# Decoder block on one core: the two attention masks loaded apart, the modulation's later pieces given to DVE or POOL in mixer B's units, staging places for x of their own

## The chip, the cores and the metric

The kernel runs on one core of a Trainium2 chip. Its time is device microseconds of one execution; the median of three runs of the kernel before is 1162.92 us (1161.84 to 1165.6). A core has TensorE (PE, with its weight loads as PEld), VectorE (DVE), ScalarE (ACT), GpSimd (POOL) and SyncE (SP), which issues the DMAs here. Each engine works through its own list of instructions in order and waits at an instruction until the semaphores that it names are reached.

## The reference

One layer of a transformer block, batch 1, 1024 tokens, width 1024, all in float32:

```python
mod = cond @ w_ada + b_ada                     # six vectors: shift, scale, gate, twice
h = rms_norm(x, g_attn_pre) * (1 + sc_a) + sh_a
proj = h @ w_in                                # q, k, v of mixer A and of mixer B
oa = banded_attention(qa, ka, va, 127, sink)   # 8 query heads, 2 key heads, window 128
ob = dilated_mixture_attention(qb, kb, vb)     # 8 heads, windows 128/1, 512/4, 2048/16
mixed = concatenate([rms_norm(oa, g_mix_a), rms_norm(ob, g_mix_b)])
x = x + gt_a * rms_norm(mixed @ w_out, g_attn_post)
h = rms_norm(x, g_mlp_pre) * (1 + sc_m) + sh_m
x = x + gt_m * rms_norm(square(relu(h @ w_up)) @ w_down, g_mlp_post)
```

`cond` is silu of the conditioning vector; q and k are partly rotated by position (rope) before the attention.

## The kernel before

Each float32 product is made of three passes on PE, with operands split into a high and a low part (`hi` by ACT, `lo` by DVE or POOL): in the projection these are L859, L860 and L862. The program is written by a planner in Python (`Sched`): steps are put in with their engine (or a choice of two), a planned duration, what they depend on, which places they take and give, and a priority. The planner keeps a clock for every engine and every DMA and writes out one fixed order for each engine. So a changed duration, priority or number of places moves instructions on all engines.

The stages, with the times of the profiled execution:

- *Prologue*, to about 60 us: norm of x, the first two of the six modulation vectors, the modulated input `hw`.
- *Input projection with attention*, to about 415 us. Six units u: 0 and 1 make the heads of mixer A, 2 to 5 those of mixer B. A unit has two halves x of 512 tokens and three chunks c (`proj_tile`: eight steps of three matmuls into `pj`). `evac` carries a chunk off: chunk 0 is rotated (DVE L755 to L758, with tables `tab` that ACT fills from `ptab`), the others are split by ACT (`hl`, L772) and DVE (L775) into a staging tile `hl`; SP scatters its rows to `kt` and `qt` (L801), some twelve DMAs a half. Values go over `vt` (ACT L823) and PE's transposes `pv` (L829). The attention runs between the matmuls of later chunks: scores `s_ps` (L1175 for A, L1120 for B), mask and maximum on DVE (L1190, L1139), exp on ACT, the scaling of the probabilities on POOL (L1207, L1151), transposes `pt_ps`, their split `ph` (ACT L1239, DVE L1243), `o_ps` (L1255, L1267) and `ot`, which SP stores to `o_dram`.
- *The rest of the modulation.* `feed_ada` puts in 24 pieces (`ada_piece`), four for each of six halves of vectors. A piece loads 512 KB of `w_ada` (`wa_st`, L992) into a staging tile and adds its two rows, times `cond`, to `ada_acc`. On POOL that takes two instructions for a row (L1007, L1008; L1003 begins a sum); a form for DVE with one instruction (L1005) exists and is used for eight more pieces in the MLP.
- *Output projection*, to about 550 us: eight blocks of 128 tokens (`out_block`): `y_ps` (L1471 to L1473), norm, times the gate (L1514), plus x (L1517, x loaded at L1420), norm, `xn` (ACT L1525), transposes `px` (L1534). `load_wo` loads `w_out` before it.
- *MLP*, to the end: seven products of half-size blocks in place of eight, eight parts; PE is filled here.

What orders the work around the change: the staging tiles of 4 KB per partition (`stage`, resource `r_stg`, five places while the projection runs) are shared by `hl`, `wa_st`, the rope rows and others. The masks of both mixers lie side by side in `masks` (1024 columns for B, 256 for A) and are loaded by one DMA (L969) when `open_attention` runs. In the output projection the staging places were tiles of the ring `ring_r`, opened by `open_h2` after the last attention step.

## Time and profile before

| | us |
|---|---|
| median of three runs | 1162.92 |
| the profiled execution | 1165.66 |
| its span, first to last instruction | 1163.9 |
| PE busy | 1116.5 |
| DVE busy | 818.9 |
| ACT busy | 639.2 |
| POOL busy | 260.9 |

The mean granted clock of PE is 0.986. The page gives an engine's busy time and its share of the span; a row of waits gives the engine and line that waited, what came last, the total, the times and the longest; a timeline row gives start, length, engine, line, instruction and, in brackets, the idle time before it. Since PE is busy for nearly all of the span, the reading goes by the few places where it is not, and by the clock that it is granted there.

### The profile page before, as it was taken

The page shows a single profiled execution, that of the slowest core. Times are in us where ns is not written, and L with a number is a line of the kernel's source. Part 1 is how long each engine was busy: PE and PEld are TensorE (multiplying, and loading weights), DVE is VectorE, ACT ScalarE, POOL GpSimd, SP SyncE. Part 2 cuts the span into 40 slices and gives each one's busy share as a digit, 9 for nine tenths or more (in the row PEclk, how much of TensorE's full clock was granted, in tenths as well). Part 3 has the DMA queues.
Part 4 walks back from the last instruction along what each step waited for, and adds up shares of the span by engine and source line. Part 5 has one row for each costly group of instructions (what it writes and reads, how often), then busy time and mean ns, then how long its engine had stood idle before and what let it go on. Part 6 is the DMA issues. An engine that isn't in the chain of part 4 may idle for free.

```text
span 1163.9 us, 15646 instructions
## 1 busy us (share of the span) xinstructions
PE 1116.5 (96%) x5416; PEld 925.9 (80%) x5416; DVE 818.9 (70%) x1380; ACT 639.2 (55%) x1105; POOL 260.9 (22%) x344
## 2 busy tenths in 40 slices
PE   9979989899999999998999999999999999999996
PEld 7768767788888777887788888888888888888885
DVE  7848667666666775668969665499653796647998
ACT  7939676445456674667666524563234732246542
POOL 2337766656562441112000000000000000000002
PEclk9989989999999989999999999999999999999998
DMA  9577847565555523564683157912369312584103
GB/s 335 175 161 168 168 108 186 114 150 114 137 117 136 137 66 131 175 205 181 228 321 123 34 188 267 331 55 91 111 216 329 113 55 73 181 302 186 37 19 145
DMA packets 90944, 185.31 MB, mean 159 GB/s; under 512 B 8432, under 2 KB 31088, under 8 KB 90864
## 3 DMA queue, kind: packets, MB, share of 16 engines
q1 hardware_dynamic: 90864, 184.30, 51.8%
q8 instruction: 43, 0.70, 0.3%
q14 instruction: 37, 0.30, 0.1%
HBM read 137.08 MB, written 28.31 MB: 142 GB/s over the span
## 4 chain that ended last, share of the span: by engine, by line
PE 69%; DVE 10%; DMA 6%; issue 5%; ACT 4%; POOL 4%; SPq 1%; DVEq 0%; POOLq 0%; ACTq 0%
PE mlp_ps L1896 16%; PE mlp_ps L1897 16%; PE mlp_ps L1895 16%; PE pj L859 3%; PE pj L862 3%; PE pj L860 3%; PE s_ps L1120 2%; DMA qt<-hl 2%; PE o_ps L1255 1%; PE pt_ps L1225 1%; PE pt_ps L1228 1%; DMA w_st<-in_w_in 1%; DMA x_sb<-in_x 1%; DVE hw L1666 1%; PE y_ps L1471 1%
## 5 line engine op out<-in xcount | busy, mean ns | idle before, releaser
L1895 PE MATMUL mlp_ps<-hw 128*128 128x512 f32 x896 | 349.7, 390 | 1.2 <-ACT hw L1657 1.2
L1896 PE MATMUL mlp_ps<-hw 128*128 128x512 f32 x896 | 348.7, 389 | 1.1 <-DVE hw L1663 1.1
L1897 PE MATMUL mlp_ps<-hw 128*128 128x512 f32 x896 | 348.6, 389 | 0.0
L1895 PEld LDWEIGHTS mlp_ps<-hw 128*128 128x128 f32 x896 | 168.2, 188 | 36.8 <-ACT hw L1657 1.6
L1896 PEld LDWEIGHTS mlp_ps<-hw 128*128 128x128 f32 x896 | 168.2, 188 | 36.6 <-DVE hw L1663 1.4
L1897 PEld LDWEIGHTS mlp_ps<-hw 128*128 128x128 f32 x896 | 168.2, 188 | 35.0
L1666 DVE TENSOR_TENSOR hw<-w,hw 128x1024 fp32r<-128x1024 f32 x96 | 114.7, 1221 | 93.5 <-ACT hw L1659 93.3
L1659 ACT CAST hw<-w 128x1024 fp32r<-128x1024 f32 x96 | 97.4, 1047 | 129.8 <-PE mlp_ps L1897 97.5
L1995 POOL TENSOR_TENSOR st<-st,nhalf 128x1 f32<-128x1 f32 x8 | 7.8, 978 | 601.9 <-DVE st L1993 601.9
L859 PE MATMUL pj<-hw,w_hl 128*128 128x512 f32 x240 | 103.8, 433 | 0.0
L862 PE MATMUL pj<-hw,w_hl 128*128 128x512 f32 x240 | 95.2, 397 | 0.0
L860 PE MATMUL pj<-hw,w_hl 128*128 128x512 f32 x240 | 94.8, 395 | 0.0
L1243 DVE TENSOR_TENSOR ph<-pt_ps,ph 128x512 fp32r<-128x512 f32 (+1 forms) x110 | 69.8, 648 | 34.8 <-ACT ph L1239 34.3
L1659 ACT CAST hw<-u 128x1024 fp32r<-128x1024 f32 x48 | 48.7, 1052 | 64.6 <-PE mlp_ps L1897 64.6
L1239 ACT CAST ph<-pt_ps 128x512 fp32r<-128x512 f32 (+1 forms) x110 | 59.4, 555 | 31.6 <-PE pt_ps L1228 26.5
L1146 ACT ACTIVATE p_sb<-p_sb,mn 128x128 f32<-128x128 f32 (+3 forms) x64 | 49.8, 778 | 37.6 <-DVE mn L1139 36.2
L1666 DVE TENSOR_TENSOR hw<-u,hw 128x1024 fp32r<-128x1024 f32 x48 | 57.1, 1220 | 18.2 <-ACT hw L1659 18.2
L1953 DVE TENSOR_TENSOR yacc<-yacc,mlp_ps 128x512 f32<-128x512 f32 x96 | 62.2, 683 | 3.3 <-PE mlp_ps L1897 3.3
L1151 POOL TENSOR_SCALAR p_sb<-p_sb,den 128x128 f32<-128x128 f32 (+3 forms) x64 | 48.5, 767 | 49.0 <-DVE den L1149 45.7
L1008 POOL TENSOR_TENSOR ada_acc<-ada_acc,wa_st 128x512 f32<-128x512 f32 x42 | 55.0, 1310 | 3.5
L862 PEld LDWEIGHTS pj<-hw,w_hl 128*128 128x128 f32 x240 | 45.5, 189 | 10.6
L1471 PE MATMUL y_ps<-hw,oh 128*128 128x512 f32 x128 | 51.7, 404 | 0.0
(205 smaller groups left out, 2014.4 us busy)
## 6 DMA issues: line engine op xcount, KB each, us to landing
hw<-s_dram SPq DMA_DIRECT2D x84, 512.0 KB
wa_st<-in_w_ada SPq DMA_DIRECT2D x32, 512.0 KB
w<-in_w_up SPq DMA_DIRECT2D x32, 512.0 KB
w<-in_w_down SPq DMA_DIRECT2D x32, 512.0 KB
s_dram<-hw SPq DMA_DIRECT2D x28, 512.0 KB
w_st<-in_w_in SPq DMA_DIRECT2D x36, 256.0 KB
x_sb<-in_x SPq DMA_DIRECT2D x16, 512.0 KB
wa<-in_w_ada SPq DMA_DIRECT2D x32, 256.0 KB
```

Of the source, the lines that this page charges most:

```text
L859: T.matmul(ps, w[:, 0, n], h[0], start=(k == 0), stop=False)
L860: T.matmul(ps, w[:, 1, n], h[0], start=False, stop=False)
L862: T.matmul(ps, w[:, 0, n], h[1], start=False, stop=(k == KC - 1))
L1239: A.copy(b["ph"][:, 0, :w], b["pt"][:, :w])
L1243: V.tensor_tensor(b["ph"][:, 1, :w], b["pt"][:, :w], b["ph"][:, 0, :w].bitcast(F32), ALU.subtract)
L1471: T.matmul(ps[:], b["oh"][:, k], wh[:, c0:c0 + 512], start=(k == 4 * m), stop=False)
L1659: A.copy(out[j][0], flat(src[j]))
L1666: V.tensor_tensor(out[j][1], flat(src[j]), out[j][0].bitcast(F32), ALU.subtract)
L1895: T.matmul(ps[m][:], sh, mh, start=starts and k == 0, stop=False, **kw)
L1896: T.matmul(ps[m][:], sh, ml_, start=False, stop=False, **kw)
L1897: T.matmul(ps[m][:], sl, mh, start=False, stop=k == 3, **kw)
L1953: e = op("DVE", t_dv(512), lambda: V.tensor_tensor(y(), y(), ps[m][:], ALU.add), [e, ml.e_y[tb, n]], gives=gives, prio=1)
```

## The change

1. The mask of A (256 columns, 128 KB) is loaded alone when the attention opens; that of B (1024 columns, 512 KB) when chunk (1, 1, 0) of the projection is put in.
2. The planner counts 1.9 times the bytes for a scatter to `kt` and `qt`.
3. The 24 pieces are put in from 1.9 units on, over 3.3 units (before: from 1.0, over 4.1), and each may go to DVE or to POOL (before: POOL).
4. `load_wo` may begin with three chunks left instead of two.
5. The four staging places of the output projection are a pool of their own (`stg2`), opened by `open_out`, which starts the output projection; the ring on the right has 20 tiles instead of 24, and `open_h2` gives no staging places any more.

```diff
@@ -440,8 +440,6 @@
     def stage(name):
-        if st.stgp is None:
-            return ring_r(name)
         return st.stgp.tile([P, 1024], F32, name=name, tag="stg")
@@ -808,7 +806,7 @@
                             posted()
-                    by = sum(a[1] * 2048 * (4 if both else 1) for a in mine)
+                    by = 1.9 * sum(a[1] * 2048 * (4 if both else 1) for a in mine)
                     e = load(f_st, by, [eh if s_ == 0 else el] + ([] if new else [e_new[u, x]]),
@@ -941,6 +939,9 @@
                 next_unit_w(u)
+            if (u, x, c) == (1, 1, 0):
+                e_mask.append(load(lambda: nc.sync.dma_start(masks[:, :1024], consts[:, CW_MB:CW_MB + 1024]), 524288,
+                                   prio=-9))
             if (u, x, c) == (2, 0, 0):
@@ -953,7 +954,7 @@
             return False
-        nonlocal kring, qring, pprob, pth, opool, adp, mask_a, mask_b, e_mask
+        nonlocal kring, qring, pprob, pth, opool, adp, masks, mask_a, mask_b, e_mask
         right0.close()
@@ -966,14 +967,14 @@
         masks = mkp.tile([P, 1280], F32, name="masks")
-        e_mask = load(lambda: nc.sync.dma_start(masks[:], consts[:, CW_MB:CW_MB + 1280]), 655360, prio=-20)
+        e_mask = [load(lambda: nc.sync.dma_start(masks[:, 1024:], consts[:, CW_MA:CW_MA + 256]), 131072, prio=-20)]
         mask_b = masks[:, 0:1024]
...
 
-    kring = qring = pprob = pth = opool = adp = mask_a = mask_b = e_mask = None
+    kring = qring = pprob = pth = opool = adp = masks = mask_a = mask_b = e_mask = None
     sc.launch += [feed_proj, open_attention]
@@ -993,7 +994,7 @@
 
-        def f_acc():
+        def f_acc(eng):
             wa = ada.raw.pop(i)[:].rearrange("p (j n) -> p j n", j=2)
@@ -1006,8 +1007,9 @@
                     G.tensor_tensor(ada.acc[:, :512], ada.acc[:, :512], wa[:, j], ALU.add)
-        e = op("DVE" if eng is V else "POOL", 1.2 if eng is V else 3.64, f_acc,
-               [el, ada.e], takes=[(r_acc or r_adacc, 1)] if jp == 0 else [], gives=[(r_stg, 1)], prio=9)
+        engs = (("DVE",), (1.3,), (lambda: f_acc(V),)) if eng is V else (
+            ("DVE", "POOL"), (1.3, 3.97), (lambda: f_acc(V), lambda: f_acc(G)))
+        e = op(*engs, [el, ada.e], takes=[(r_acc or r_adacc, 1)] if jp == 0 else [], gives=[(r_stg, 1)], prio=9)
         ada.e = e
@@ -1059,8 +1061,8 @@
     def feed_ada():
-        if st.d > 1.0 + ada.i * 4.1 / NADA and ada.i < NADA:
-            ada_piece(ada.i, G, lambda: adp.tile([P, 512], F32, name="ada_acc", tag="ada_acc", bufs=1), lambda: px.tile([P, 512], F32, name="ada_ps", tag="x"), r_x)
+        if st.d > 1.9 + ada.i * 3.3 / NADA and ada.i < NADA:
+            ada_piece(ada.i, None, lambda: adp.tile([P, 512], F32, name="ada_acc", tag="ada_acc", bufs=1), lambda: px.tile([P, 512], F32, name="ada_ps", tag="x"), r_x)
             ada.i += 1
@@ -1139,7 +1141,7 @@
                                            mn[:, 0:1] if m else BIG, ALU.add, ALU.min, mn[:, m:m + 1])
-                last_mn = op("DVE", t_dv(cw) + (AP_DV if m else 0), f_max, [e, e_mask] + ([last_mn] if m else []), gives=[(r_s, 1)], prio=1)
+                last_mn = op("DVE", t_dv(cw) + (AP_DV if m else 0), f_max, [e, e_mask[1]] + ([last_mn] if m else []), gives=[(r_s, 1)], prio=1)
 
@@ -1194,7 +1196,7 @@
                                  scale=-1.0, accum_out=b["den"][:, h:h + 1])
-                em = op("DVE", t_dv(256 - k0) + 0.16, f_max, [e, es, e_mask], gives=[(r_s, 1)] if hh else [], prio=1)
+                em = op("DVE", t_dv(256 - k0) + 0.16, f_max, [e, es, e_mask[0]], gives=[(r_s, 1)] if hh else [], prio=1)
                 ea.append(op("ACT", t_sb(256 - k0) + 2 * AP_COST, f_exp, [em], prio=1))
@@ -1331,7 +1333,7 @@
 
-        if len(todo_dense) > 2 or ada.i < NADA:
+        if len(todo_dense) > 3 or ada.i < NADA:
             return False
@@ -1362,13 +1364,14 @@
         ph2.left = pool("ring_l", 10)
-        st.stgp = None
         r_stg.free.clear()
...
         ph2.junk = pool("junk2", 1).tile([P, D], BF16, name="junk2")
+        st.stgp = pool("stg2", NSTG2)
+        r_stg.give(sc.clk["PE"], NSTG2)
         ph2.tb = 0
@@ -1381,8 +1384,7 @@
         rightv.close()
-        ph2.right = pool("ring_r", 24, "right")
-        r_stg.give(sc.clk["PE"], NSTG2)
+        ph2.right = pool("ring_r", 20, "right")
         r_raw.give(sc.clk["PE"], 10)
```

What this does to the order, at three places on which the prediction rests. First SP, where it has loaded the first weights and begins to scatter the keys and queries of unit 0, half 0. Before:

```order
L528 DMA w_st<-in_w_in 128x512 x6
L969 DMA masks<-in_consts 128x1280
L528 DMA w_st<-in_w_in 128x512
L992 DMA wa_st<-in_w_ada 128x2x512
L801 DMA kt<-hl 64x2x512 x2
L801 DMA qt<-hl 8x4x512 x4
```

Now:

```order
L526 DMA w_st<-in_w_in 128x512 x6
L970 DMA masks<-in_consts 128x256
L526 DMA w_st<-in_w_in 128x512
L799 DMA kt<-hl 64x2x512 x2
L799 DMA qt<-hl 8x4x512 x4
```

The load of the modulation is gone from ahead of `kt`, and the masks' load is a fifth as wide. The other 1024 columns stand now behind both halves' scatters and two loads of weights of unit 1. On PE three `pj` matmuls and the first four `pv` now stand ahead of the first scores instead of behind them.

Second SP again, at the scatter of unit 1, half 1. The number behind a name tells tiles apart: `hl_1457`, `hl_1598` and `hl_1748` are the staging tiles of chunks 0, 1 and 2 before. Before:

```order
L801 DMA qt_1520<-hl_1457 8x4x512 x4
L528 DMA w_st_1577<-in_w_in 128x512
L1312 DMA o_dram3_113<-ot_1531 64x2x128 x2
L1048 DMA gate_d0_80<-gate_st_1412 128x512
L801 DMA qt_1520<-hl_1598 24x4x512
L801 DMA qt_1520<-hl_1598 8x4x512
L992 DMA wa_st_1624<-in_w_ada 128x2x512
L801 DMA qt_1520<-hl_1598 24x4x512
L801 DMA qt_1520<-hl_1598 8x4x512
L528 DMA w_st_1665<-in_w_in 128x512
L992 DMA wa_st_1741<-in_w_ada 128x2x512
L801 DMA qt_1520<-hl_1748 16x4x512
```

Now, where `hl_1470`, `hl_1569` and `hl_1694` are those tiles:

```order
L799 DMA qt_1527<-hl_1470 8x4x512 x4
L799 DMA qt_1527<-hl_1569 24x4x512
L799 DMA qt_1527<-hl_1569 8x4x512
L526 DMA w_st_1598<-in_w_in 128x512
L1314 DMA o_dram3_113<-ot_1571 64x2x128 x2
L799 DMA qt_1527<-hl_1569 24x4x512
L799 DMA qt_1527<-hl_1569 8x4x512
L526 DMA w_st_1647<-in_w_in 128x512
L993 DMA wa_st_1656<-in_w_ada 128x2x512
L799 DMA qt_1527<-hl_1694 16x4x512
```

The first of all `wa_st` loads now stands behind the last store of chunk 1; before, two stood in this stretch, one between the stores of chunk 1.

Third the pieces of the modulation in unit 2. POOL before, where `w_hl` is the low part of a weight tile and `p_sb` are probabilities:

```order
L542 TENSOR_TENSOR w_hl<-w_st,w_hl 128x512
L1007 TENSOR_SCALAR wa_st<-wa_st,cond 128x512
L1008 TENSOR_TENSOR ada_acc<-ada_acc,wa_st 128x512
L1007 TENSOR_SCALAR wa_st<-wa_st,cond 128x512
L1008 TENSOR_TENSOR ada_acc<-ada_acc,wa_st 128x512
L1166 COPY p_sb<-nsink 128x4
L1207 TENSOR_SCALAR p_sb<-p_sb,den_1769 128x256 x4
```

DVE now, at its second piece (`mn` is the row maximum with the mask, `den` the sum):

```order
L1192 ISA p_sb,mn_1932<-s_ps,masks,nsink 128x256
L1192 ISA mn_1932 128x1
L1201 RECIPROCAL den_1933<-den_1933 128x4
L1006 SCALAR_TENSOR_TENSOR ada_acc<-wa_st,cond,ada_acc 128x512 x2
L1245 TENSOR_TENSOR ph<-pt_ps,ph 128x512
L1192 ISA p_sb,mn_2050<-s_ps,masks,nsink 128x256
L1192 ISA mn_2050 128x1
```

Four instructions on POOL have become two on DVE, between the steps of the attention. Of the 24 pieces 19 are on DVE and five on POOL.

In the output projection SP's load of x for block 0 stands right behind the load of that block's attention output (`o_sb`); before, it stood behind six more stores and a second `o_sb`. PE's order in the MLP is the same.

## The prediction

> **What bounds the kernel now.** I began with the page's busy times, then the stages (windows), then the waits of TensorE, and last the timeline at each long wait.
>
> ```profile
> PE 1116.5 (96%) x5416; PEld 925.9 (80%) x5416; DVE 818.9 (70%) x1380; ACT 639.2 (55%) x1105; POOL 260.9 (22%) x344
> ```
>
> TensorE (PE) has work for 96% of the span. So the change can win only idle time of PE and half-clock time of PE. The stages say where those are; the columns are the stretch, its length, the busy time of PE, PEld, DVE, ACT and POOL (with counts), the granted clock, the DMA share and GB/s.
>
> ```profile
> 155.00:385.00 230.00, 223.99 (x1265) 189.01 (x1264) 152.51 (x389) 130.21 (x284) 133.98 (x149) 1.00 0.57 133
> 60.00:155.00 95.00, 81.64 (x430) 67.47 (x429) 57.43 (x166) 61.50 (x169) 59.92 (x101) 0.92 0.76 161
> ```
> ```profile
> 570.00:600.00 30.00, 30.00 (x134) 24.86 (x133) 22.43 (x22) 18.34 (x26) 0.00 (x0) 1.00 0.90 337
> ```
>
> The MLP (from 570 us) leaves no gap in such a row. Units 0 and 1 (60 to 155 us) lose 95 - 81.64 = 13.4 us, and the clock of 0.92 costs about 7 more; units 2 to 5 (155 to 385 us) lose 6 us. The waits of PE name the causes (total, times, longest):
>
> ```profile
> PE s_ps L1175 <- DMA kt<-hl: 7.3, 1, 7.3
> PE px L1534 <- ACT xn L1525: 5.7, 3, 3.1
> PE pv L829 <- ACT tab L719: 5.2, 1, 5.2
> PE pv L829 <- DVE ot L1291: 3.2, 2, 2.8
> ```
>
> The change touches the first three of them: the first scores' wait for scattered keys and queries (7.3), the wait behind ACT at 146 us (5.2), and one of the three waits for `xn` in the output projection.
>
> **The masks and the first scores.** SP's timeline (start, length, instruction) shows the scatter behind a load of the modulation (the masks' load is the DMA but one before it), and PE's what waits for it; the third fence has the DMA share and rate in three stretches of 2 us, the fourth the granted clock:
>
> ```profile
> 65.03 0.44 SPq L992 DMA_DIRECT2D wa_st<-in_w_ada  x1
> 67.65 1.78 SPq L801 DMA_DIRECT2D kt<-hl  x2
> 69.49 8.23 SPq L801 DMA_DIRECT2D qt<-hl  x10
> ```
> ```profile
> 77.25 0.39 PE L862 MATMUL pj<-hw,w_hl 128*128 128x512 f32 x1
> 84.97 1.94 PE L1175 MATMUL s_ps<-kt,qt 128*128 128x128 f32 x8 [7.33 <-DMA kt<-hl]
> ...
> 88.09 0.63 PE L859 MATMUL pj<-hw,w_hl 128*128 128x512 f32 x1
> ...
> 89.51 0.69 PE L829 MATMUL pv<-head,vt 64*128 64x64 f32 x4
> 90.12 1.74 PE L1175 MATMUL s_ps<-kt,qt 128*128 128x256 f32 x8
> ```
> ```profile
> 66.00:68.00 2.00, 2.00 (x11) 1.65 (x10) 1.92 (x4) 1.74 (x4) 1.48 (x2) 1.00 1.03 380
> 72.00:74.00 2.00, 2.00 (x10) 1.65 (x9) 0.14 (x1) 0.00 (x0) 1.92 (x3) 1.00 0.58 93
> 78.00:80.00 2.00, 0.00 (x0) 0.00 (x0) 0.00 (x0) 0.44 (x1) 0.00 (x0) 1.00 0.99 153
> ```
> ```profile
> 81.08:84.49 3.41, 0.00 (x0) 0.00 (x0) 0.63 (x1) 0.00 (x0) 0.00 (x0) 0.50 0.77 124
> 84.49:87.91 3.42, 2.94 (x11) 2.78 (x12) 3.34 (x10) 1.10 (x2) 0.43 (x1) 0.50 0.66 134
> 87.91:91.32 3.41, 3.41 (x13) 2.45 (x13) 0.64 (x5) 2.52 (x11) 2.41 (x6) 0.50 0.78 136
> ```
>
> The order now puts only 128 KB of mask ahead of the scatter. Mask B (128 x 1024 x 4 bytes) and the first `wa_st` (as much) leave the queue: 1.05 MB, at the 380 GB/s of 66 to 68 us 2.8 us of transfer. That is the most the scatter can come earlier. The least is nothing: the last scatter is issued at 69.49 + 8.23 = 77.7 us whatever lies ahead, and at 72 to 74 us the DMA engines were only 0.58 busy, waiting for issue. I take 2.0, nearer to the upper end since at 78 to 80 us they were full (0.99) and still worked off the queue.
>
> Second, PE's order now has three more `pj` matmuls and the four `pv` ahead of the first scores. They stood behind them at half clock: 89.51 - 88.09 = 1.4 for the three and 90.12 - 89.51 = 0.6 for the four, so 1.9 to 2.0 us, now hidden in the wait. I count 1.9.
>
> Third, the clock. It was 0.50 from 81.08 to 91.32 us: full speed came only after a window in which PE had 3.41 of 3.41 us. If the scores start at about 83, the window 84.49 to 87.91 is full and the next is fast: 3.41/2 = 1.7 won. I take 1.1, as the wait stays over 4 us and the drop itself remains. **Sum: -2.0 - 1.9 - 1.1 = -5.0 us**, from -1.9 (transfers no earlier) to -6.4. In these rows the drop goes with a long idle stretch of PE. The Trainium skill, TensorE: Matmul & The Clock Gate, Part 1, says that the gate watches a free-running window of about 3.4 us and halves the clock after an idle one; the rows agree (steps of 3.41 us). By that rule a wait shortened below a window would keep the clock and this part would be some 2 us better still.
>
> **Mask B and the modulation's pieces out of unit 1.** ACT's waits from 120 to 156 us, SP's timeline, the chain and the clock:
>
> ```profile
> ACT hl L772 <- DMA qt<-hl: 5.1, 1, 5.1
> ```
> ```profile
> 135.49 0.44 SPq L992 DMA_DIRECT2D wa_st<-in_w_ada  x1
> ```
> ```profile
> 137.66 9.39 DMA qt<-hl
> ```
> ```profile
> 149.35:152.76 3.41, 0.93 (x5) 0.81 (x6) 2.73 (x9) 3.36 (x11) 3.24 (x5) 0.50 0.49 125
> 152.76:156.17 3.41, 3.41 (x14) 3.12 (x14) 1.50 (x6) 1.09 (x4) 3.37 (x8) 0.50 0.38 89
> ```
>
> ACT's `hl` of unit 1 needs a stage place. Five exist and the order has two `wa_st` loads among that half's stores, the first of them above, so it waits for the scatter of the chunk before (9.39 us, with 512 KB loads in the same queue). Everything behind it on ACT is late by 5.1 us, and PE with it (5.2), then PE works 0.93 + 3.41 = 4.3 us at half clock, which is 2.2 us lost. In the new order no `wa_st` is issued until the last scatter of that chunk, and the `hl` takes a place that the chunk before the last gave back. At best the whole 5.2 + 2.2 = 7.4 goes; what is late next is ACT's own queue. **I take -6.5**, range -7.4 to -3. Mask B's load (512 KB) now stands in unit 1, ahead of that unit's scatter; the scores that need it are in unit 2, tens of microseconds later, so I cost it at nothing. If it delays that scatter, the price is its transfer, 1.4 us at 380 GB/s.
>
> **The pieces on DVE.** POOL did 24 pieces of two steps each in units 1 to 5 and DVE does 19 of them now, at units 2 to 5. The rows of before, by line (min/median/max ns); the DVE row is of the pieces that it does in the MLP:
>
> ```profile
> L1007 POOL TENSOR_SCALAR wa_st<-wa_st,cond x42: 686/698/1129, 72.4 to 338.4; 128x512 f32<-128x512 f32 x42
> L1008 POOL TENSOR_TENSOR ada_acc<-ada_acc,wa_st x42: 1269/1296/1615, 73.2 to 339.2; 128x512 f32<-128x512 f32 x42
> ...
>   DMA wa_st<-in_w_ada: 34.5, 9
> ```
> ```profile
> L1005 DVE SCALAR_TENSOR_TENSOR ada_acc<-wa_st,cond,ada_acc x14: 746/752/753, 630.8 to 784.4; 128x512 f32<-128x512 f32 x14
> ```
> ```profile
> DVE ot L1291 <- DMA o_dram<-ot: 3.8, 1, 3.8
> ```
>
> 19 x 2 x 0.75 = 28.5 us at most come to DVE, and 19 x 2 x (0.70 + 1.30) = 76 us leave POOL. From 155 to 385 us DVE was busy 152.5 of 230; it will be 181, or 79%. That is cover, but DVE keeps its order: behind a piece stand, in the new order, `ot`, `ph` and the masked scores; PE waits for `ph`, ACT for the scores, and both wait out a piece (1.5 us), and its load too if that is late. POOL sat 34.5 us, in 9 waits, for these loads, at little cost to PE. How a DVE wait reaches PE one row pair shows: DVE waited 3.8 for a DMA, PE 2.8 for that `ot` (0.74 of it). Bounds: -2 (of the 6 us that PE lost there a freer POOL, which scales the probabilities for the transposes, wins back a third), +8 (11 us of DVE delays reach PE at 0.74). **I take +2**: the loads are now placed after the scatters, which get 1.9 times the planned cost, and PE lost only 6 us there in all.
>
> Now the row on which a rule bears that speaks against the move:
>
> ```profile
> L542 DVE TENSOR_TENSOR w_hl<-w_st,w_hl x14: 674/692/1247, 18.2 to 309.5; 128x512 fp32r<-128x512 f32 x14
> ```
>
> Some DVE steps with two SBUF inputs took up to 1247 ns for 692, while the median is undisturbed. The Trainium skill, SBUF — State Buffer, Who interferes with whom, says that a DVE instruction with two SBUF inputs and a GpSimd instruction that reads SBUF shut each other out for the whole instruction; the pieces are of that kind. What it would do here is the fifth rival.
>
> **Places for x.** In block 0 of the output projection the sum with x waits for x:
>
> ```profile
> 447.46 1.27 DVE L1514 SCALAR_TENSOR_TENSOR y_sb<-y_sb,st,gate_a 128x1024 f32<-128x1024 f32 x1
> ...
> 453.38 1.22 DVE L1517 TENSOR_TENSOR y_sb<-y_sb,x_sb 128x1024 f32<-128x1024 f32 x1 [1.67 <-DMA x_sb<-in_x]
> ```
> ```profile
> 458.45 1.09 PE L1534 MATMUL px<-head,xn 128*128 128x128 f32 x8 [2.17 <-ACT xn L1525]
> ```
>
> `y_sb` is ready at 448.73, x comes at 453.3, PE stands 2.17 us for what follows. With places from the start of the output projection, SP loads x right behind the block's `o_sb`, ahead of six stores that it used to follow. The 4.6 us go, and PE's 2.2 us with them; next late is ACT's `xn`, covered by the matmuls of block 1. **-2.2**, range 0 to -2.3. That `load_wo` may start one chunk earlier and that the second ring has 20 tiles I cost at nothing: PE's order in the MLP is the same, and the MLP rows have no gap.
>
> **Sum.** -5.0 - 6.5 - 2.2 + 2.0 = -11.7. The profiled execution took 1165.66 (span 1163.9 and 1.8 around it), 2.7 above the median of the three runs; its waits are all in the program's order, so I take the difference from the median: 1162.92 - 11.7 = **1151.2 us**.
>
> **The rivals.**
> 1. *Slower: DVE takes over POOL's waits for `wa_st`.* 34.5 x 19/24 = 27.3 us of DVE waits in units 2 to 5, at 0.74: 20.2 us of PE against 13.7 gained, **1169.4 us**. It decides from 13.7/0.74 = 18.5 us of DVE waits on. For it: DVE's first step of each piece waits for the load itself. Against: DMA share there is only 0.57, and the pieces stand where the plan has the load landed. Chance 0.08.
> 2. *The scatter itself bounds the first scores*: of part one only the 1.9 us of moved work stay, 1162.9 - 1.9 - 6.5 - 2.2 + 2 = **1154.3**. For it: 0.58 DMA share while SP issues. 0.20.
> 3. *The lack of stage places comes back* in units 2 to 5, where now all 24 loads ask for the same five places, and a load that waits for one holds on SP the scatter behind it: one more stall like that at 146 us, 7.4: **1158.6**. 0.15.
> 4. *x comes no earlier* (its load stands behind stores or waits for the memory of the projection's pools): **1153.4**. 0.10.
> 5. *Shared access of DVE and POOL.* POOL keeps 134 - 76 = 58 us of 230, so 38 x 0.25 = 10 collisions of about 0.4 us, 4 us of DVE, at 0.74 3 us: **1154.2**. At worst each of the 38 would wait out 0.70: 27 us, which is rival 1. Against: a median of 692 beside 674. 0.05.
>
> My forecast has 0.42. The range: below, all terms at their good ends (-6.4 - 7.4 - 2.3 - 2 = -18.1) give 1144.8; above, rivals 2 and 3 together give 1161.7, of which I leave out the last part, and rival 1: **1144 to 1160**. A measurement of this kernel can tell 0.3%, 3.5 us, from no change: the median of before spans 1161.84 to 1165.6. Faster by more than that (under 1159.4): forecast, rivals 2, 4, 5 and most of 3, 0.82; the same 0.10; slower 0.08 (rival 1).
>
> **What would show it.** First scores near 83 us and half clock ended by about 88; no wait of `hl` on ACT near 146 us and no half clock there; x landed before `y_sb` of block 0 is ready, and PE without a gap at `px` of block 0; DVE near 180 us busy in units 2 to 5, with waits for `wa_st` of a few microseconds in all, and PE still losing about 8 us there. Wrong it is if DVE's waits for `wa_st` exceed 18 us, or if a new PE gap with half clock stands in units 2 to 5.

## The result, and the profile after

| | before | after |
|---|---|---|
| median, us | 1164.26 (1161.84 to 1167.14, 4 runs) | 1177.37 (1174.86 to 1178.04, 4 runs) |
| profiled execution, us | 1165.66 | 1176.72 |
| its span, us | 1163.9 | 1174.9 |

The ratio is 1.0108, with a 95% interval of 1.0077 to 1.0138. The change makes the kernel slower by 1.1%, where the forecast was 11.7 us faster.

The page's busy times and two stages, in the columns of the windows shown before:

```profile
PE 1124.4 (96%) x5416; PEld 930.6 (79%) x5416; DVE 842.5 (72%) x1412; ACT 634.6 (54%) x1092; POOL 210.0 (18%) x293
```
```profile
60.00:155.00 95.00, 81.47 (x415) 67.10 (x414) 56.75 (x163) 56.58 (x156) 40.51 (x83) 0.89 0.66 123
155.00:385.00 230.00, 218.68 (x1215) 183.25 (x1214) 165.22 (x406) 122.15 (x272) 95.02 (x111) 0.99 0.62 147
```

POOL lost 51 us of work and DVE gained 24; that way round was meant. But PE did 15 matmuls fewer between 60 and 155 us than before (415 for 430) and 50 fewer between 155 and 385 (1215 for 1265). So the stage that was to win 11.5 us won nothing, and units 2 to 5 lost time.

Where exactly is seen when the same matmul is looked up in both traces. The table gives its start before, and how much later it starts after and in each experiment told below (one profiled execution each, worked out from matmul starts). The landmarks, counted from 0, are: the 48th `pj` (in unit 0), the 144th (unit 1, half 1), the 168th (unit 2 begins), the 624th (unit 5), the first and the 126th `y_ps` (output projection), the first and the 224th `mlp_ps`.

```
               pj 48  pj 144  pj 168  pj 624  y_ps 0  y_ps 126 mlp 0  mlp 224
before (start)  91.7   140.1   157.9   356.2   416.6    467.0  533.9    593.3
after           -2.3    +1.4    +1.7   +12.4   +12.4    +11.1  +10.8    +11.7
e1_noread       -3.6    +1.6    +2.2    +2.1    +1.5     -0.2   -0.5     -0.3
e2_short        -3.7    -2.3    -2.0    -3.8    -4.5     -5.3   -5.6     -4.9
e3_both         -2.4    +2.7    +2.9    -1.9    -2.5     -3.6   -3.9     -1.7
e4_pool         -4.0    +1.6    +2.2     0.0    +3.5     +3.7   +3.4     +3.4
e5_w2           -3.5    +1.5    +4.2   +12.7   +15.8    +15.6  +15.3    +16.3
e6_xplaces      -0.7    -0.3    -4.3    -0.3    -0.1     -0.8   -1.0     +0.7
e7_late         -3.4    -2.2    -3.6   +21.1   +33.2    +27.2  +27.3    +28.3
e8_masks        +0.5   +11.6    +4.5   +13.7   +16.9    +17.1  +17.1    +18.0
e9_w2both       -3.5    +1.5    +1.5    -4.3    -1.1     -0.3   -0.6     -0.5
e10_noada       -2.2    +4.0    +1.9    +2.5    +5.6     +6.1   +5.9     +6.8
e11_nomask      -3.8    -4.5    -3.0    +6.5    +6.9     +6.9   +6.6     +7.6
e12_f19x       -11.2    -4.7    -6.0    -7.1    -7.7     -8.9   -9.2     -9.0
```

The rows are single executions. e6_xplaces has the order of before on every engine up to 410 us, and yet it is 4.3 us ahead at the 168th `pj` and level again at the 624th. The last column differs from the distance of the medians by up to 4 us (e12_f19x: -9.0 here, 5.0 by the medians; its profiled execution was the fastest of ten). So a difference of less than some 4 us in one row says nothing by itself, and the ratios below decide. At the 48th `pj` the orders themselves differ by up to 20 matmuls.

After is 2.3 us ahead in unit 0, 1.7 behind when unit 2 begins, loses 10.7 from there to unit 5 (12.4 - 1.7), wins 1.6 back by the start of the MLP and ends 11 to 12 behind. The longest waits of PE, in the form shown before (the lines are two further down or up than before: `ph` is L1245, `xn` L1527, `tab` L717):

```profile
PE o_ps L1257 <- DVE ph L1245: 6.5, 7, 1.5
PE ptab L715 <- ACT tab L717: 4.6, 1, 4.6
PE px L1536 <- ACT xn L1527: 3.9, 3, 3.0
PE pv L827 <- ACT vt L821: 3.8, 2, 3.5
PE o_ps L1269 <- DVE ph L1245: 3.3, 3, 1.6
```

The wait of 7.3 for the scatter is gone from the top, but `vt` (3.8) is new there, and so is the wait for `ph`: 6.5 + 3.3 us where it was 2.7 + 1.4. The wait behind ACT near 146 us (4.6 for 5.2) is still there under another name.

**The first scores.** SP's, ACT's and PE's timelines of after, and the DMA (last three columns: granted clock, DMA share, GB/s):

```profile
67.60 1.39 SPq L799 DMA_DIRECT2D kt<-hl  x2
69.43 7.68 SPq L799 DMA_DIRECT2D qt<-hl  x10
```
```profile
78.64 0.59 ACT L770 ACTIVATE hl<-acc 64x512 fp32r<-64x512 f32 x1 [7.50 <-DMA qt<-hl]
79.98 0.58 ACT L821 COPY vt<-acc 64x512 f32<-64x512 f32 x1 [0.75 <-DVE hl L773]
```
```profile
80.62 0.69 PE L827 MATMUL pv<-head,vt 64*128 64x64 f32 x4 [3.55 <-ACT vt L821]
...
86.29 1.94 PE L1177 MATMUL s_ps<-kt,qt 128*128 128x128 f32 x8 [2.13 <-DMA qt<-hl]
```
```profile
76.00:82.00 6.00, 2.45 (x11) 1.74 (x10) 0.68 (x1) 1.54 (x3) 0.00 (x0) 0.84 0.97 129
82.00:86.00 4.00, 2.16 (x6) 1.15 (x4) 1.24 (x2) 0.00 (x0) 0.00 (x0) 0.50 0.64 87
```

The load of the modulation is gone from ahead of the scatter, and the first scores start at 86.29, against 84.97 before. With nothing but scatters issued from 67.6 us on, the queue moved 129 GB/s at a share of 0.97, then 87. So a scatter can fill the DMA engines by itself at a third of the 380 GB/s that I had divided by: what lay ahead of it was not what it waited for. And the `pv` that were now to fill the wait need `vt`, which on ACT stands behind an `hl` that the same scatter held for 7.50 us. PE stood 3.55 + 2.13 us in place of 7.33. The half clock lasted as long as before, and PE worked through more of it:

```profile
80.05:83.46 3.41, 2.84 (x9) 2.32 (x10) 0.00 (x0) 0.89 (x2) 0.00 (x0) 0.50 0.96 114
83.46:86.88 3.42, 1.29 (x5) 0.62 (x4) 2.08 (x3) 0.00 (x0) 0.00 (x0) 0.50 0.54 106
86.88:90.29 3.41, 3.41 (x13) 2.93 (x13) 2.10 (x10) 2.62 (x10) 1.42 (x2) 0.50 0.74 114
```

That is 7.54 us of work at half speed, against 2.94 + 3.41 = 6.35 in the three windows of before.

**146 us.** ACT's waits from 136 to 150 us, its timeline, SP's and PE's, and the clock:

```profile
ACT w_hl L535 <- DMA w_st<-in_w_in: 7.4, 2, 6.2
```
```profile
145.18 0.62 ACT L535 CAST w_hl<-w_st 128x512 fp32r<-128x512 f32 x1 [6.19 <-DMA w_st<-in_w_in]
```
```profile
136.04 0.39 SPq L526 DMA_DIRECT2D w_st<-in_w_in  x1
```
```profile
146.92 1.11 PE L715 MATMUL ptab<-head,rows 128*128 128x128 f32 x4 [4.62 <-ACT tab L717]
```
```profile
144.90:148.31 3.41, 1.39 (x6) 1.29 (x7) 1.88 (x3) 2.17 (x4) 0.00 (x0) 0.50 0.78 193
148.31:151.73 3.42, 3.42 (x10) 2.65 (x9) 1.67 (x3) 1.79 (x3) 0.00 (x0) 0.50 0.79 223
```

`hl` waits for no place any more. The next instruction on ACT that needs the same queue does: a weight load of 256 KB, issued at 136.04 between the scatters, is used at 145.18, 9.1 us later, and the wait, PE's gap and both half-clock windows are much like those of before.

**Units 2 to 5.** The same stretch of work in both kernels, from the 168th to the 624th `pj`, first before, then after:

```profile
157.90:356.20 198.30, 192.72 (x1087) 162.14 (x1086) 130.67 (x337) 110.97 (x250) 121.53 (x137) 1.00 0.59 133
```
```profile
159.60:368.60 209.00, 197.68 (x1088) 164.97 (x1087) 153.04 (x373) 108.79 (x246) 87.55 (x100) 0.98 0.63 145
```

The same number of matmuls takes 209.00 us for 198.30. PE's idle time is 11.3 for 5.6, and its busy time 5.0 more. Most of that is two windows of half clock that were not there before, each behind a window in which PE was idle for part of it:

```profile
264.37:267.78 3.41, 2.06 (x13) 1.52 (x12) 3.29 (x10) 1.35 (x5) 0.28 (x1) 1.00 1.01 119
267.78:271.20 3.42, 3.42 (x12) 2.83 (x12) 1.98 (x9) 2.63 (x9) 1.43 (x4) 0.50 0.68 216
...
315.57:318.99 3.42, 1.63 (x14) 1.53 (x14) 3.42 (x5) 0.07 (x1) 2.47 (x3) 1.00 0.00 1
318.99:322.40 3.41, 3.41 (x13) 2.93 (x11) 1.57 (x4) 1.06 (x2) 1.90 (x2) 0.50 0.63 216
```

DVE's waits for the pieces' loads from 140 to 400 us, then one piece on DVE's timeline, and PE's instruction behind it:

```profile
DVE ada_acc L1006 <- DMA wa_st<-in_w_ada: 12.8, 9, 3.1
...
DVE ada_acc L1004 <- DMA wa_st<-in_w_ada: 0.8, 1, 0.8
```
```profile
177.22 1.54 DVE L1006 SCALAR_TENSOR_TENSOR ada_acc<-wa_st,cond,ada_acc 128x512 f32<-128x512 f32 x2 [3.09 <-DMA wa_st<-in_w_ada]
178.68 0.68 DVE L1245 TENSOR_TENSOR ph<-pt_ps,ph 128x512 fp32r<-128x512 f32 x1
```
```profile
179.41 0.50 PE L1269 MATMUL o_ps<-ph,v_hl 128*128 128x512 f32 x1 [1.63 <-DVE ph L1245]
```

DVE stood 3.09 us for the load and worked 1.54 us on the piece; `ph`, which came behind both, is what PE waited for.

**x.** DVE's and PE's timelines in block 0 of the output projection:

```profile
460.38 1.27 DVE L1516 SCALAR_TENSOR_TENSOR y_sb<-y_sb,st,gate_a 128x1024 f32<-128x1024 f32 x1
461.68 1.22 DVE L1519 TENSOR_TENSOR y_sb<-y_sb,x_sb 128x1024 f32<-128x1024 f32 x1
```
```profile
467.54 1.09 PE L1536 MATMUL px<-head,xn 128*128 128x128 f32 x8 [0.36 <-ACT xn L1527]
```

The sum follows its `y_sb` with no wait, and PE's stop of 2.17 us is 0.36.

### The profile page after: what moved, and what is told of

Its sections match the earlier page's. It is cut to its first block, busy times and chain, and to the rows that moved or that the text cites. A ratio compares the mean times of both kernels' runs of the same rounds, so it can differ in the third digit from the quotient of the medians.

```text
span 1174.9 us, 15618 instructions
## 1 busy us (share of the span) xinstructions
PE 1124.4 (96%) x5416; PEld 930.6 (79%) x5416; DVE 842.5 (72%) x1412; ACT 634.6 (54%) x1092; POOL 210.0 (18%) x293
## 4 chain that ended last, share of the span: by engine, by line
PE 64%; DVE 12%; DMA 10%; issue 5%; ACT 5%; POOL 2%; SPq 1%; DVEq 0%; POOLq 0%; ACTq 0%
PE mlp_ps L1898 16%; PE mlp_ps L1899 16%; PE mlp_ps L1897 16%; DMA wa_st<-in_w_ada 4%; DMA qt<-hl 2%; PE pj L857 2%; PE pj L858 2%; PE pj L860 2%; PE s_ps L1122 1%; DVE ph L1245 1%; SPq L799 1%; PE o_ps L1257 1%; DVE hw L1668 1%; DMA w_st<-in_w_in 1%; PE o_ps L1269 1%
## 5 line engine op out<-in xcount | busy, mean ns | idle before, releaser
L857 PE MATMUL pj<-hw,w_hl 128*128 128x512 f32 x240 | 105.7, 441 | 0.0
L858 PE MATMUL pj<-hw,w_hl 128*128 128x512 f32 x240 | 96.4, 402 | 0.0
L860 PE MATMUL pj<-hw,w_hl 128*128 128x512 f32 x240 | 96.4, 402 | 0.0
L1245 DVE TENSOR_TENSOR ph<-pt_ps,ph 128x512 fp32r<-128x512 f32 (+1 forms) x110 | 69.5, 646 | 33.5 <-ACT ph L1241 33.3
L1006 DVE SCALAR_TENSOR_TENSOR ada_acc<-wa_st,cond,ada_acc 128x512 f32<-128x512 f32 x46 | 39.5, 860 | 16.0 <-DMA wa_st<-in_w_ada 15.0
```

The costliest lines, as they stand in the source:

```text
L857: T.matmul(ps, w[:, 0, n], h[0], start=(k == 0), stop=False)
L858: T.matmul(ps, w[:, 1, n], h[0], start=False, stop=False)
L860: T.matmul(ps, w[:, 0, n], h[1], start=False, stop=(k == KC - 1))
L1245: V.tensor_tensor(b["ph"][:, 1, :w], b["pt"][:, :w], b["ph"][:, 0, :w].bitcast(F32), ALU.subtract)
```

## The experiments

The theory at the start: in units 2 to 5 DVE's waits for the loads reach PE through `ph` (rival 1 of the prediction at a smaller size). Its rivals: the work of the pieces on DVE alone, with collisions with POOL, does it; or the order that the new planning wrote does it, whatever the pieces cost. Each kernel was timed against the kernel before on its own chip.

| | edit | median, us | ratio to before (95%) |
|---|---|---|---|
| e1_noread | after, pieces don't use the load | 1167.34 | 1.0002 (0.9982 to 1.0022) |
| e2_short | after, pieces 8 columns wide | 1164.56 | 0.9994 (0.9981 to 1.0006) |
| e3_both | both edits | 1162.03 | 0.9971 (0.9958 to 0.9985) |
| e4_pool | after, pieces on POOL alone | 1168.68 | 1.0028 (1.0014 to 1.0042) |
| e5_w2 | after, unit 2's weights not from the load | 1181.39 | 1.0138 (1.0113 to 1.0162) |
| e6_xplaces | before with part 5 | 1164.70 | 0.9984 (0.9968 to 1.0000) |
| e7_late | after, pieces planned later | 1195.49 | 1.0260 (1.0231 to 1.0289) |
| e8_masks | before with part 1 | 1183.54 | 1.0151 (1.0126 to 1.0175) |
| e9_w2both | e5 with e3 | 1166.13 | 1.0005 (0.9988 to 1.0022) |
| e10_noada | after without part 3 | 1171.53 | 1.0049 (1.0030 to 1.0068) |
| e11_nomask | after without part 1 | 1172.83 | 1.0061 (1.0031 to 1.0092) |
| e12_f19x | before with parts 2 and 5 | 1161.54 | 0.9954 (0.9933 to 0.9974) |

### The pieces on DVE: the wait without the work, the work without the wait

In the first three kernels every engine has the same list of instructions as in after.

**e1_noread** takes the wait away and leaves the work: DVE's pieces multiply columns of `hw`, which has long been there, instead of the loaded `w_ada`. The loads still run. (The modulation is then made of other numbers.)

```diff
...
-                    V.scalar_tensor_tensor(ada.acc[:, :512], wa[:, j], cj, ada.acc[:, :512], ALU.mult, ALU.add)
+                    V.scalar_tensor_tensor(ada.acc[:, :512], hw[:, j, 0, :512].bitcast(F32) if i < NADA else wa[:, j], cj, ada.acc[:, :512], ALU.mult, ALU.add)
```

> The changed kernel with the same order on every engine, but the 19 pieces on DVE in units 2 to 5 read a part of the modulated input that is long there in place of their loaded tile (so the modulation's values are others); the loads are still issued. So DVE does the same work and waits for no load. Theory A (DVE's waits for late loads, 13.6 us in the trace, at 0.74 about 10 us of PE): about 1167 us. Theory B (DVE's 28 us of added work delays the attention steps behind it): about 1177, as changed. Theory C (the loads come later and denser and delay scatters and weights): about 1177.

Measured: 1167.34, and from unit 2 to unit 5 a change of -0.1 us against before, where after had lost 10.7. The same piece on DVE's timeline, and the same stretch of work:

```profile
174.55 1.61 DVE L1006 SCALAR_TENSOR_TENSOR ada_acc<-hw,cond,ada_acc 128x512 f32<-128x512 f32 x2
176.88 0.69 DVE L1245 TENSOR_TENSOR ph<-pt_ps,ph 128x512 fp32r<-128x512 f32 x1 [0.72 <-ACT ph L1241]
```
```profile
160.10:358.30 198.20, 194.30 (x1088) 162.27 (x1087) 152.35 (x373) 108.54 (x246) 88.20 (x99) 1.00 0.65 153
```

DVE is as busy as in after (152.35 for 153.04), and `ph` waits for its input from ACT, not behind the piece. So the work alone does not make the loss, and neither do its collisions with POOL: the mean of its 32 long steps (those that add to a sum) is 937 ns here and 908 in after.

**e2_short** does the reverse: the pieces still wait for their loads, and then add 8 columns of 512 (the rest of the modulation is left out; the six steps that begin a sum keep their width).

```diff
-                    V.scalar_tensor_tensor(ada.acc[:, :512], wa[:, j], cj, ada.acc[:, :512], ALU.mult, ALU.add)
+                    V.scalar_tensor_tensor(ada.acc[:, :(8 if i < NADA else 512)], wa[:, j, :(8 if i < NADA else 512)], cj, ada.acc[:, :(8 if i < NADA else 512)], ALU.mult, ALU.add)
```

> The changed kernel with the same order on every engine, but the 32 accumulating steps of the pieces on DVE are 8 columns wide in place of 512 (so most of the modulation's sums are left out); they still wait for their loads. Theory A (waits): about 1176, nearly as changed. Theory B (work): about 1167. Theory C (loads): about 1177.

Measured: 1164.56; units 2 to 5 win 1.8 us against before. Yet DVE waits longer for the loads than in after (waits of DVE from 140 to 400 us, then the same piece, then the stretch of work):

```profile
DVE ada_acc L1006 <- DMA wa_st<-in_w_ada: 14.9, 9, 3.3
...
DVE ada_acc L1004 <- DMA wa_st<-in_w_ada: 0.8, 1, 0.8
```
```profile
173.46 0.49 DVE L1006 SCALAR_TENSOR_TENSOR ada_acc<-wa_st,cond,ada_acc 128x8 f32<-128x8 f32 x2 [3.00 <-DMA wa_st<-in_w_ada]
173.86 0.68 DVE L1245 TENSOR_TENSOR ph<-pt_ps,ph 128x512 fp32r<-128x512 f32 x1
```
```profile
155.90:352.40 196.50, 192.71 (x1088) 162.46 (x1088) 136.63 (x373) 108.04 (x246) 84.79 (x99) 1.00 0.66 155
```

15.7 us of waits, a wait of 3.00 at the very piece where after had 3.09, and no loss. So the theory of the waits falls as it stood, and so does that of the work. What after has at this piece and neither of these has is a wait and then 1.5 us of work in one lump ahead of `ph`.

**e3_both** has the edits of both, neither wait nor work (and the parts of the computation left out that they name).

> Both edits together: the pieces on DVE neither wait for their loads nor take more than some tenths of a microsecond (most of the modulation's sums are left out and the rest reads other values). Theories A and B: about 1166, what is left above the kernel before is units 0 and 1 (1.4 us) less the output projection (1.5 us). Theory C: about 1177.

Measured: 1162.03; units 2 to 5 win 4.8 us. The same stretch of work:

```profile
160.80:354.30 193.50, 191.94 (x1088) 162.68 (x1088) 137.92 (x373) 108.08 (x246) 84.50 (x99) 1.00 0.67 157
```

With it the four kernels form a square, and the loss between `pj` 168 and 624 reads, against e3: work alone +4.7, wait alone +3.0, both +15.5. The last is 7.8 more than the sum of the two. By the ratios it is the same: +0.0031, +0.0023, and +0.0137 for both. That is 0.0083 more than the sum, where the four intervals together, taken as independent, leave about 0.004. All four have one order, so the order alone is ruled out too.

PE's idle time in this stretch shows it place by place. The table has the longest gaps, by the number of the matmul in PE's list, in us (a dash is under 0.1); e5, told below, has after's order, waits and work, and repeats it:

| matmul, waits for | after | e5_w2 | e1, work alone | e2, wait alone | e3, neither |
|---|---|---|---|---|---|
| 824, `ph` | 1.63 | 1.97 | - | 0.49 | - |
| 999, `ot` | 1.81 | 1.15 | 0.88 | 1.13 | 0.87 |
| 1141, `ph` | 1.53 | 1.14 | - | 1.06 | - |
| 1259, `ph` | 1.26 | 1.25 | 1.25 | - | - |
| 1530, `v_hl` | 1.79 | 1.39 | 0.12 | - | - |
| all others | 3.30 | 3.98 | 1.65 | 1.11 | 0.69 |
| sum | 11.32 | 10.88 | 3.90 | 3.79 | 1.56 |

The excess over e3 is 9.8 us in after, 2.3 for the work alone and 2.2 for the wait alone. DVE's order has slack for either, not for one after the other: at 824 and 1530 the gap needs both. At 1141 the wait does most of it, at 1259 the work alone, in two pieces in a row whose steps are long beside POOL.

Half clock comes on top, in part by luck. The window before 267.78 has its 1.35 us of idle time (3.41 - 2.06) from the gap at 1259. e1 has the same gap; there it lies across two windows, with PE busy for 2.39 and 3.09 of 3.41 us, and no half clock follows. After has two half-clock windows in this stretch and e5, with nearly the same gaps, one (183.32).

**e4_pool** lets the planner put the pieces on POOL alone, with the later feeding kept; the order changes with it.

```diff
-            ("DVE", "POOL"), (1.3, 3.97), (lambda: f_acc(V), lambda: f_acc(G)))
+            ("POOL",), (3.97,), (lambda: f_acc(G),))
```

> The changed kernel with all 24 pieces on POOL, as before, still put in from 1.9 units on over 3.3; the planner makes a new order of it. Theories A and B: DVE is free of pieces, so about 1165 to 1168. Theory C: the loads are as late and dense as in the changed kernel, about 1175.

Measured: 1168.68, about 0.8% better than after by the two ratios; units 2 to 5 win 2.2 us against before. POOL then waits for the loads even longer than DVE did in after (waits of POOL from 140 to 400 us: 19.7 us in 9 for L1008 and 11.4 in 2 for L1004), and PE hardly notices. POOL had room for the wait and the work; DVE had not. The later feeding by itself is not the cause.

**e7_late** was to remove the waits by letting the planner believe in a slower load, so that the pieces stand later.

```diff
-        el = load(f_load, 524288, takes=[(r_stg, 1)], prio=20)
+        el = load(f_load, 524288 if eng is V else 2097152, takes=[(r_stg, 1)], prio=20)
```

> The changed kernel with the planned cost of the 24 loads of the modulation four times as high, so that the planner puts their pieces later, behind the landing; 18 or so pieces stay on DVE. Theory A/B (wait and work of the pieces together delay DVE's queue): DVE waits for these loads under 4 us in all, units 2 to 5 lose about 3 to 5 us instead of 11, so about 1168. Theory A alone: 1166. If only the work counts: 1175.

Measured: 1195.49, the slowest of all. No wait of DVE for these loads is left, but the staging places are now held longer in the plan, the order around `hl` and `ot` is another, and PE stands 5.0 us in all at each of two new places (for DVE's `hl` at L756, at most 2.9 at once; for `ot` at L1293, at most 2.6) and gets half clock in four stretches of units 2 to 5. It doesn't tell the theories apart; it shows how much an order can cost by itself.

### The masks and the wait at 146 us

**e8_masks** is the kernel before with part 1 alone.

```diff
-        e_mask = load(lambda: nc.sync.dma_start(masks[:], consts[:, CW_MB:CW_MB + 1280]), 655360, prio=-20)
+        e_mask = [load(lambda: nc.sync.dma_start(masks[:, 1024:], consts[:, CW_MA:CW_MA + 256]), 131072, prio=-20)]
...
```

> The kernel before with the first part of the change alone: the masks apart, mask B in unit 1. If the scatter's own rate bounds the first scores, as the changed kernel's trace says (its last piece landed at 86.1 us with nothing else in the queue): first scores between 84 and 87 us and 1.000 of before, within 0.003. If transfers ahead of it did bound them: first scores near 83 us and 0.997.

Measured: 1183.54, 1.5% slower than before. Its first scores, and its waits of PE from 76 to 155 us:

```profile
85.74 1.94 PE L1178 MATMUL s_ps<-kt,qt 128*128 128x128 f32 x8 [5.02 <-DMA qt<-hl]
```
```profile
PE o_ps L1270 <- DVE ph L1246: 5.3, 1, 5.3
PE s_ps L1178 <- DMA qt<-hl: 5.3, 2, 5.0
```

512 KB of mask less ahead of the scatter, and the scores come at 85.74, not earlier than before's 84.97. In unit 1 this order loses 11 us (table: +0.5, then +11.6), with a wait for `ph` that before has not; by the 168th `pj` it is 4.5 behind, since before has its stall at 146 us in between, and units 2 to 5 lose 9.2 more. So the masks' part brings nothing at its own place, and its order costs elsewhere.

**e11_nomask**, after without part 1, is the other side.

```diff
-        e_mask = [load(lambda: nc.sync.dma_start(masks[:, 1024:], consts[:, CW_MA:CW_MA + 256]), 131072, prio=-20)]
+        e_mask = load(lambda: nc.sync.dma_start(masks[:], consts[:, CW_MB:CW_MB + 1280]), 655360, prio=-20)
...
```

> The changed kernel without its first part: one load of both masks ahead of the first scatter. If the masks apart cost time here too (as they did alone): under 1172. If only the pieces on DVE do: 1177 within 3.

Measured: 1172.83, about 0.5% better than after by the middles of the two ratios, whose intervals overlap. The first scores, with the full masks ahead of the scatter again:

```profile
84.73 1.94 PE L1174 MATMUL s_ps<-kt,qt 128*128 128x128 f32 x8 [0.59 <-DMA qt<-hl]
```

They are no later than with a fifth of the masks ahead: after and its variants with the same order start theirs between 84.89 (e2) and 86.34 (e5). By the 144th `pj` this kernel is 4.5 us ahead of before and after is 1.4 behind. DVE still waits 11.8 us for the pieces' loads (L1003, 9 times), and units 2 to 5 still lose 9.5 us (6.5 + 3.0): wait and work on DVE cost much the same in another order.

**e10_noada** is after without part 3: the pieces are fed from 1.0 units on, on POOL.

```diff
-        if st.d > 1.9 + ada.i * 3.3 / NADA and ada.i < NADA:
+        if st.d > 1.0 + ada.i * 4.1 / NADA and ada.i < NADA:
...
```

> The changed kernel without its third part: all pieces on POOL, put in from 1.0 units on over 4.1, as before; masks apart, the scatter's planned cost, load_wo and the places for x as changed. Theory: the loss of the change is the pieces on DVE, so about 1164 to 1168. Rival (the masks apart fill unit 1's burst of transfers, as in the run with the masks alone): about 1180.

Measured: 1171.53. Units 2 to 5 lose 0.6 us instead of 10.7; the rest is what part 3 costs there, as far as another order can show it. It isn't back at before's time since it loses elsewhere: 1.9 us before unit 2 (the first scores start at 87.05, after a wait of 7.21 us for `qt`) and 3.1 between the 624th `pj` and the first `y_ps`.

**e5_w2** keeps the order of after and takes away the load that ACT waited for at 146 us: unit 2's weights are split from columns of `hw` (unit 2 is then projected with other weights).

```diff
-            A.copy(w[:, 0], w_raw[a][:])
+            A.copy(w[:, 0], hw[:, a[1], 0, :512].bitcast(F32) if a[0] == 2 else w_raw[a][:])
...
```

> The changed kernel with the same order on every engine, but the weights of unit 2 are split from a part of the modulated input instead of from their loaded tiles (so that unit's heads are other values); the loads are still issued. Theory W (in unit 1 the wait of ACT for a weight load that queues behind the scatter has taken the place of its wait for a staging place; nothing else is late there): the 4.6 us wait of PE at 142 to 147 us and the half clock after it go, together about 7 us, so about 1170. Rival (something else is late at the same place, the scatter's own landing or a staging place): PE's wait stays within 2 us of what it was, about 1177.

Measured: 1181.39, not faster than after. ACT's wait is gone, and a third has taken its place, DVE's for the first `wa_st` (waits of DVE from 140 to 156 us, then PE):

```profile
DVE ada_acc L1004 <- DMA wa_st<-in_w_ada: 7.1, 1, 7.1
```
```profile
154.69 0.69 PE L827 MATMUL pv<-head,vt 64*128 64x64 f32 x4 [6.55 <-DVE ot L1309]
```

`ot` stood behind that piece on DVE. **e9_w2both** takes this wait away too (e5 with the edits of e3, and the parts left out that both name).

> The changed kernel with the same order on every engine; unit 2's weights are split from a part of the modulated input, and the pieces on DVE neither wait for their loads nor take long (other values, most of the modulation's sums left out). Theory Q (in unit 1 the loads behind the scatter land about 9 us late, and PE stops for whichever in-order engine meets one of them first): with both waiters freed the stall of PE between 140 and 156 us and its half clock go, 7 us below the run with the pieces freed alone, about 1155. Rival (a third waiter, the scattered rows themselves): 1160 to 1162.

Measured: 1166.13, above both expected times and above e3 (1162.03). PE gets further and then stops again, probably for the scattered rows themselves; the clock follows:

```profile
154.58 0.71 PE L1177 MATMUL s_ps<-kt,qt 128*128 128x256 f32 x4 [4.25 <-DMA o_dram<-ot]
```
```profile
152.12:155.54 3.42, 0.96 (x9) 0.99 (x9) 0.02 (x1) 0.00 (x0) 1.37 (x2) 1.00 0.77 224
155.54:158.96 3.42, 3.42 (x14) 2.96 (x13) 0.00 (x0) 0.84 (x2) 3.34 (x5) 0.50 0.02 6
```

The row puts the wait down to a store in the same queue; the last `qt` of that half was issued at 145.88 behind two 512 KB loads and landed at 154.24. That the scores wait for these rows is argued from that landing, not shown. So from 146 to 155 us four instructions wait in turn for one busy queue: `hl` for a place (before), `w_hl` for weights (after), a piece for its load (e5), the scores for their rows (e9). Each wait that is taken away uncovers the next, at most 8 us later. At the 168th `pj` e9 is 1.4 us ahead of e3; it loses 3.2 against before between the 624th `pj` and the first `y_ps`, with half clock from 408.1 to 421.8.

### x, and a better version

**e6_xplaces** is the kernel before with part 5 alone.

```diff
...
+        st.stgp = pool("stg2", NSTG2)
+        r_stg.give(sc.clk["PE"], NSTG2)
...
-        ph2.right = pool("ring_r", 24, "right")
-        r_stg.give(sc.clk["PE"], NSTG2)
+        ph2.right = pool("ring_r", 20, "right")
```

> The kernel before with the fifth part of the change alone, the staging places of the output projection in a pool of their own. My term: PE's 2.2 us at the first block's transposes go, 0.998 of before. Rival (the transposes then wait for the norm's chain on ACT and DVE, or the gain is given back at the MLP's start): 1.000.

Measured: 1164.70, a ratio of 0.9984 (0.9968 to 1.0000): 1.9 us at the middle, with no change at the interval's end.

**e12_f19x** is before with parts 2 and 5, which seemed the useful ones: 1.9 times the planned bytes for a scatter, and the places for x.

```diff
-                    by = sum(a[1] * 2048 * (4 if both else 1) for a in mine)
+                    by = 1.9 * sum(a[1] * 2048 * (4 if both else 1) for a in mine)
...
```

> The kernel before with the scatter's planned cost 1.9 times as high and the places for x apart, nothing else. If the planned cost makes the order fit the transfers better, 1158 to 1162; if it does not matter, as the places for x alone, 1163 to 1165.

Measured: 1161.54, a ratio of 0.9954 (0.9933 to 0.9974): faster than both kernels. Its first scores, and the stretch from 60 to 155 us:

```profile
83.83 1.08 PE L1173 MATMUL s_ps<-kt,qt 128*128 128x128 f32 x8 [2.35 <-DMA qt<-hl]
```
```profile
60.00:155.00 95.00, 86.61 (x465) 71.67 (x464) 60.66 (x178) 64.12 (x177) 64.83 (x110) 0.95 0.70 167
```

All masks and a 512 KB `wa_st` still lie ahead of the scatter, and its first scores are the earliest of the kernels told here. PE waits 2.35 us there, not 7.33, because a plan that counts the scatter as longer puts more `pj` ahead of the scores: PE has such work until 81.5 us, where it ended at 77.6 in before. PE did 35 matmuls more in this stretch than before (465 for 430). This profiled execution was the fastest of ten, 5.5 us under the median, and e12's interval overlaps that of e6 (part 5 alone), so how much of the 0.5% is the planned cost stays open.

## Why the prediction was wrong, point by point

By the table, forecast and measurement lie 23.4 us apart at the 224th `mlp_ps` (-11.7 and +11.7): 13.2 of it in points 1 and 2 (-11.5 forecast, +1.7 found at the start of unit 2), 8.7 in point 3, the rest in point 4 and the head of the MLP.

1. *Masks and first scores, -5.0: failed.* The step that failed is "the most the scatter can come earlier" by transfer, 2.0 taken of 0 to 2.8. The low end was true, as rival 2 had it: the scatter's own rate (129 and 87 GB/s) sets its end, and the first scores came no earlier with less ahead of it (after, e8) and no later with more (e11, e12). The 0.99 share at 78 to 80 us, which I read as a queue of loads being worked off, is no sign of that: after shows 0.97 with scatters alone. The 1.9 us of moved work shrank too, since the `pv` wait for `vt`, which waits for the scatter (3.55). The clock: 1.2 us more of work at half speed, so 0.6 lost and not 1.1 won. What was left, 2.3 us at the 48th `pj` (part of it order: at the 400th matmul of PE it is 0.6), was gone by the 144th: the next scores waited 1.9 us at 100.2, by the trace for a weight load in the same queue, and another window of half clock followed, 100.53 to 103.94.

2. *`hl` at 146 us, -6.5: failed.* The named wait did go, as predicted. "What is late next is ACT's own queue" was written and costed at nothing; next late on it was a load behind the same scatter, of the same length (6.19 for 5.1). From the 144th `pj` to the 168th the change is +0.3. The term was also sized from one execution: in e6, with before's order, this wait of `hl` is 2.9 us, PE's is 2.9 for 5.2, and no half clock follows. Where I counted 3 to 7.4 us, 2.9 were there to win in that execution.

3. *Pieces on DVE, +2: right in sign, far too small.* +10.7 was measured, above the upper bound of 8. Bounding by "11 us of DVE delays at 0.74" was near in the delays (13.6) but counted the waits alone, and treated the 1.5 us of work as cover. e1 and e2 show that each alone nearly fits into the slack and both together don't. Two windows of half clock came on top, 6.8 us of work at half speed and so 3.4 lost; the bound had no term for them, and where they fall is in part luck. Rival 1 named the place and the releaser rightly, and its point of decision (18.5 us of waits) wrongly: 13.6 us did it in after, and 15.7 cost nothing against before in e2.

4. *x, -2.2: right in the mechanism*, with 1.6 measured between the first `y_ps` and the first `mlp_ps`, and 1.9 as e6's middle, whose interval reaches no change. The sum waits for nothing, and PE's wait for `xn` in the output projection fell from 2.6 to 0.9 us (440 to 550 us). About 0.9 was given back at the head of the MLP (+10.8 to +11.7).

The sum as measured: +1.7 (to the start of unit 2) + 10.7 - 1.6 + 0.9 = +11.7 at the 224th `mlp_ps`, and 11.0 at the span's end, where the forecast was -11.7. The other rivals: of the third, no wait of `hl` for a place is among ACT's longest waits in units 2 to 5, and the lack of places did not come back; the fourth is ruled out by x; the fifth's collisions did come: 32 steps at a mean of 908 ns for a median of 752, 5.0 us in sum, where 4 had been estimated. POOL kept 95 us of work from 155 to 385 us, not the 58 counted. e1 has these collisions too and loses nothing against before, though PE's gap of 1.25 us at matmul 1259 stands behind them in both:

```profile
L1006 DVE SCALAR_TENSOR_TENSOR ada_acc<-wa_st,cond,ada_acc 128x512 f32<-128x512 f32 x32 | 29.0, 908 | 13.6 <-DMA wa_st<-in_w_ada 12.8
```

Of the signs listed beforehand, "a new PE gap with half clock in units 2 to 5" is the one that came true (267.78 and 318.99); "waits over 18 us" was not needed for it.

What stays open: how fast a scatter runs in a given execution. With one and the same order its last piece for the first scores landed at 86.1 us in after and e1 and at 84.7 in e2; no run here shows why. Also open is which instruction of e8's order first costs it the 11 us in unit 1; only the waits are shown. And no kernel has part 2 or part 4 alone.

## What to carry to other kernels

Before counting what a transfer wins when loads ahead of it go, read its rate in a stretch where nothing else is in the queue: if it fills the DMA engines there by itself, the gain is nothing, and more work planned ahead of its user is what helped here. A stall read from one execution may be half as long in the next: with one order the wait at 146 us was 5.2 us in one and 2.9 in another. For a wait that is to be removed on an in-order engine, list what that engine needs next from the same queue; the wait moves there. Work with a late input that moves onto an engine with slack must be priced as wait plus work in one lump ahead of the next instruction that somebody waits for: each alone may cost little, and a test of each alone shows whether they add.

## What the runs showed of the hardware

Half clock can follow a window of 3.41 us in which PE was idle for only part of it: 2.06 of 3.41 us busy and 1.63 of 3.42 were each followed by a window at 0.50, and 0.96 of 3.42 in e9. It need not follow: in before PE was busy for 1.76 us of the window from 210.79, and the next stayed at 1.00. Counted over the fourteen traces, on the grid of each one's clock changes and without start and end, full-speed windows with PE busy for up to 1.5 us were all followed by half clock (55 of 55), those with 1.5 to 2.4 us in 21 cases of 97, those with more never. Full speed can come back after a window that is not quite full, too: in e1 PE was busy for 2.93 us of the half-clock window from 81.01, and the next was at 1.00 (the prediction had read from before's rows that it took 3.41 of 3.41). The Trainium skill, TensorE: Matmul & The Clock Gate, Part 1, speaks of one idle window as the condition; these rows show that a partly busy one can be enough, so the measurement decides. Its step of about 3.4 us agrees with every row.

Scatters from SBUF to SBUF of 2 KB pieces ran at 87 to 129 GB/s with the DMA engines up to 0.97 busy, where the loads at 66 to 68 us had reached 380. DMA share tells that the queue works, not that it moves much.

A DVE step beside a POOL step can last until that one ends, however short it is by itself: in e2 two steps of 8 columns took 0.98 and 1.22 us and ended at 255.00 and 256.26, where POOL's steps ended at 254.99 and 256.23; the next, with POOL idle, took 0.23.
